# Normed tokens and their differences for the block products, moved from ScalarE and GpSimd to the vector engine, with five instead of four old-way blocks in each ConvFFN

## The chip, the cores and the metric

The kernel runs on one core of one Trainium2 chip. The metric is the device time of one execution in microseconds (us). The core's engines are TensorE (PE in the rows; PEld are its weight loads), the vector engine (DVE), ScalarE (ACT), GpSimd (POOL) and SyncE (SP), on whose queue the transfers are issued. Each engine works through its own instructions in a fixed order and waits on semaphores for the others.

## The reference, cut to what matters

Two decoder layers run over 592 tokens (16 meta tokens, 64 of samples, 512 of the prompt) of width 1024: a mixer and a ConvFFN in each. The change touches the ConvFFN:

```
u, gate = split(rms_norm(x, norm_ffn) @ w_in, 2)       # w_in: 1024 x 5632
conv = conv_b + sum(padded[:, j:j+t] * conv_w[j])      # 3 taps over time
x = x + (silu(conv) * gate) @ w_out                    # w_out: 2816 x 1024
```

## The kernel before, in words

Features lie on the 128 partitions and tokens along the free axis, so x is eight tiles of 128x592. A product in fp32 is made of three products of a high and a low part (`h`, `xl` of the tokens; `wh`, `wl` of the weights). A weight's parts are made by ScalarE (L295) and the vector engine (L299) from a tile `wr` that a transfer has filled; `wr` has two buffers, `wh` and `wl` three each.

`ffn` runs over 22 blocks of 128 features. Each makes `u` and `gate` for its features, then convolution, silu and gating (`activate`, a chain of steps that alternates between ScalarE and the vector engine).

- The *old way* (`in_block`): `dense` for u and for gate, each 8 chunks x 3 parts x 2 halves of the tokens = 48 matmuls, 96 in a block, over raw tokens; the norm's factor per token, `rb`, is multiplied in afterwards, when `up` reads the products of u (L563, L568, tile `ub`) and `gt` those of gate (L771).
- The *seven-product way* (`strassen_block`): weights and tokens are cut into quadrants, and seven products of sums and differences of quadrants take 7 x 4 x 3 = 84 matmuls. They need the normed tokens `xn` and their differences, split into high and low parts: `b11h`, `b11l`, `b2h`, `b2l` of single quadrants (`split_alone`), and of the differences (the tiles `h` and `xl` again, which the raw tokens have left by then).

Blocks 0 to `NOLD - 1` run in the old way, since the operands of the other have to be made first. Before, `NOLD` is 4: during block 1 `norm_chunk` makes `xn` (ScalarE scales by the gain, GpSimd multiplies by `rb`, L625 and L626), during block 2 `split_alone` splits single quadrants and `differences` has GpSimd subtract (L653 to L656), and after the gate products of block 3 `split_differences` splits all eight differences in one run (L662, L663). GpSimd also copies a few edge columns of each block's `ub` (`up_edges`, L545 to L549; L548 in layer 0 only) and its last columns (L554, L555); the first tap on ScalarE (L586) waits for them.

PSUM tiles of the old way come from a pool of two (`mm`), and so do the `ac` tiles of the seven-product way and those of the output projection (`out_pair`, 48 matmuls, one after each of the blocks 4 to 19): a product can start when the last but one has been read. A scheduler puts each engine's instructions in order, by the order in which the code issues them and by when their operands should be there.

Of the kernel before, what the change touches and what calls it, by code (L numbers as in the profile page):

```python
# [9 lines left out]
F32 = mybir.dt.float32  # L10
F32R = mybir.dt.float32r
I32 = mybir.dt.int32
U8 = mybir.dt.uint8
AF = mybir.ActivationFunctionType
ALU = mybir.AluOpType
# [8 lines left out]
NT = NMETA + NSAM + NP  # L24
# [75 lines left out]
def trunk_kernel(ctx: ExitStack, tc: tile.TileContext, I, O):  # L100
    nc = tc.nc
    V, S, G, T = nc.vector, nc.scalar, nc.gpsimd, nc.tensor
# [3 lines left out]
    ap = ctx.enter_context(tc.tile_pool(name="ap", bufs=1))  # L106
# [10 lines left out]
    def matmul(out, lhsT, rhs, **kw):  # L117
        n = 1
        for d in rhs.shape[1:]:
            n *= d  # L120
        m = lhsT.shape[1]
        clock[0] += max(n, 64) / 2.4 + 3 if rhs.dtype == F32R else max(2 * n, 2 * m, 64) / 1.2
        T.matmul(out, lhsT=lhsT, rhs=rhs, **kw)  # L123
# [38 lines left out]
    def tmp(name, n=NT, dt=F32):  # L162
        return tp.tile([128, n], dt, name=name, tag="t", bufs=4)
# [7 lines left out]
    def px(name):  # L171
        return pp.tile([128, 512], F32, name=name, tag="px", bufs=4)

    def mm(name):
        return pp.tile([128, 1024], F32, name=name, tag="mm", bufs=2)
# [28 lines left out]
    x = [None] * 8  # L204
    state = {"x": "xa", "h": "xb", "ssq": {}}

    def xslot(c, name, dt=F32):
        return ap.tile([128, NT], dt, name=f"{name}{c}", tag=f"{state[name]}{c}")
# [147 lines left out]
    def got(ws):  # L356
        return [sp.get() for sp in ws]
# [25 lines left out]
    def dense(ws, acts, c0=0, hooks=None, span=None):  # L383


        off, mid = OFF[c0]
        halves = [(c0, mid), (mid, NT)] if span is None else [span]
        if span is not None:
            off = -span[0]
        ps = [mm("dp") if span is None else px("dq") for _ in ws]  # L390
        nk = len(acts)
        for k in range(nk):
            xh, xl = acts[k]
            for p, (hi, lo) in zip(ps, ws):
                for i, (ww, xx) in enumerate(((hi, xh), (hi, xl), (lo, xh))):
                    for a, b in halves:
                        matmul(p[:, off + a:off + b], lhsT=ww[:, k, :], rhs=xx[:, a:b], start=k == 0 and i == 0,
                               stop=k == nk - 1 and i == 2)
            if hooks and k in hooks:
                hooks[k]()  # L400
            yield
        return ps, off
# [4 lines left out]
    def acts_x():  # L407
        return [state[c] for c in range(8)]
# [120 lines left out]
    def ffn(l, next_gain, spans=(None,)):  # L529
# [21 lines left out]
        def up_state(fc, ub):  # L551
            cvo = env["cvo"]
            ubs = ub[:, 0:100].rearrange("p (s i) -> p s i", i=10)
            G.tensor_copy(cvo[:, 0:2, fc], ub[:, 612:614])  # L554
            G.tensor_copy(cvo[:, 2:18, fc].rearrange("p (b j) -> p b j", j=2), ubs[:, 2:10, 8:10])  # L555
# [3 lines left out]
        def up(fc, pu, off):  # L559
            rb = state["rb"]  # L560
            ub = tmp("ub", 614)
            ubs = ub[:, 0:100].rearrange("p (s i) -> p s i", i=10)
            V.tensor_tensor(out=ubs[:, s0:, 2:10], in0=pu[:, off + h0:off + 80].rearrange("p (s i) -> p s i", i=8),  # L563
                            in1=rb[:, h0:80].rearrange("p (s i) -> p s i", i=8), op=ALU.mult)
            if l == 1:
                V.tensor_tensor(out=ub[:, 100:102], in0=pu[:, off + 14:off + 16], in1=rb[:, 14:16], op=ALU.mult)
            up_edges(fc, ub)
            V.tensor_tensor(out=ub[:, 102:614], in0=pu[:, off + P0:off + NT], in1=rb[:, P0:NT], op=ALU.mult)  # L568
            up_state(fc, ub)
            return ub  # L570
# [46 lines left out]
        a0 = 0 if l == 0 else 12  # L617
        n = (NT - a0) // 2
        h1, h2 = slice(a0, a0 + n), slice(a0 + n, NT)
        xn, ops = [None] * 8, {}  # L620

        def norm_chunk(c):
            g = vec[:, V_NFFN + 8 * l + c:V_NFFN + 8 * l + c + 1]
            xn[c] = ap.tile([128, NT], F32, name=f"xn{c}", tag=f"b{'hl'[c % 2]}{4 + c // 2}")
            S.activation(xn[c], x[c], AF.Copy, scale=g)  # L625
            G.tensor_tensor(out=xn[c], in0=xn[c], in1=state["rb"], op=ALU.mult)  # L626

        def split_alone(c):

            x_ = xn[c]  # L630
            if c < 4:
                if c % 2 == 0:
                    for i in "hl":
                        ops["1", i, c // 2] = tp.tile([128, 2, 296], F32R, name=f"b11{i}", tag="gate", bufs=4)
                hi, lo = (ops["1", i, c // 2][:, c % 2, 0:n] for i in "hl")
                S.activation(hi, x_[:, h1], AF.Copy, scale=-1.0)
                V.scalar_tensor_tensor(out=lo, in0=x_[:, h1], scalar=-1.0, in1=hi.bitcast(F32), op0=ALU.mult,  # L637
                                       op1=ALU.subtract)
                ops["B11", c] = (hi, lo)
            else:  # L640
                if c % 2 == 0:
                    ops["2", "h", c // 2] = ap.tile([128, 2, 592], F32R, name="b2h", tag="v", bufs=2)
                    ops["2", "l", c // 2] = tp.tile([128, 2, 592], F32R, name="b2l", tag="st", bufs=2)
                hi, lo = (ops["2", i, c // 2][:, c % 2, 0:2 * n] for i in "hl")
                S.copy(hi, x_[:, a0:NT])
                V.tensor_tensor(out=lo, in0=x_[:, a0:NT], in1=hi.bitcast(F32), op=ALU.subtract)  # L646
                ops["B21", c - 4] = (hi[:, 0:n], lo[:, 0:n])
                ops["B22", c - 4] = (hi[:, n:2 * n], lo[:, n:2 * n])

        def differences(c):  # L650

            p, q = xn[c], xn[c + 4]
            G.tensor_tensor(out=p[:, h1], in0=p[:, h1], in1=p[:, h2], op=ALU.subtract)  # L653
            G.tensor_tensor(out=p[:, h2], in0=p[:, h2], in1=q[:, h2], op=ALU.subtract)
            G.tensor_tensor(out=q[:, h2], in0=p[:, h1], in1=q[:, h2], op=ALU.add)
            G.tensor_tensor(out=q[:, h1], in0=q[:, h2], in1=q[:, h1], op=ALU.subtract)  # L656

        def split_differences():
            for c in range(8):
                hi = xslot(c, "h", F32R)  # L660
                lo = ap.tile([128, NT], F32R, name=f"xl{c}", tag=f"xl{c}")
                S.copy(hi[:, 0:2 * n], xn[c][:, a0:NT])  # L662
                V.tensor_tensor(out=lo[:, 0:2 * n], in0=xn[c][:, a0:NT], in1=hi[:, 0:2 * n].bitcast(F32),  # L663
                                op=ALU.subtract)
                a, b = ("T1", "T3") if c < 4 else ("T4", "T2")
                ops[a, c % 4] = (hi[:, 0:n], lo[:, 0:n])
                ops[b, c % 4] = (hi[:, n:2 * n], lo[:, n:2 * n])

        def strassen_block(fc):

# [74 lines left out]
            r = lambda: raw_weights([v], True)  # L745
            return (lambda: [Split(4, 256, r())], body)

        NOLD = 4

        def in_block(fc):  # L750
            def body(ww):
                hooks = (None, None)
                if fc == 0:
                    setup()
                    hooks = ({7: norm_rows}, {4: norm_bcast})
                ww = got(ww)
                if fc == 1:
                    hooks = ({k: lambda k=k: norm_chunk(k // 2 + 4 * (k % 2)) for k in range(8)}, None)
                elif fc == 2:
                    hooks = ({k: lambda k=k: split_alone(k // 2 + 4 * (k % 2)) for k in range(8)},  # L760
                             {4 + k: lambda k=k: differences(k) for k in range(4)})
                (pu,), off = yield from dense(ww[0:1], acts_x(), c0, hooks[0])
                if fc > 0:
                    ub = up(fc, pu, off)
                (pg,), off = yield from dense(ww[1:2], acts_x(), c0, hooks[1])
                if fc == 0:
                    ub = up(fc, pu, off)
                if fc == NOLD - 1:
                    split_differences()
                gt = tmp("gt")  # L770
                V.tensor_tensor(out=gt[:, h0:], in0=pg[:, off + h0:off + NT], in1=state["rb"][:, h0:], op=ALU.mult)  # L771
                activate(fc, ub, gt)
                while later:
                    step_later()

            return (lambda: weights([cols(w_in, fc * 128)], [cols(w_in, DFF + fc * 128)]), body)
# [7 lines left out]
        acts = [None] * NFC  # L784
        block = lambda fc: in_block(fc) if fc < NOLD else strassen_block(fc)
        blocks = [block(fc) for fc in range(4)]
# [919 lines left out]
```

## Time and profile before

| | |
|---|---|
| median of 3 runs | 1619.34 us (1617.38 to 1619.64) |
| the profiled execution | 1614.75 us |
| its span, first to last instruction | 1612.6 us |
| mean granted clock of TensorE | 0.986 of full speed |
| busy: PE, DVE, ACT, POOL | 95%, 72%, 46%, 16% |

Busy shares are averages over the whole span; what a stage waits for is read from that stage. A granted clock of 1.00 is the 2.4 GHz level, 0.50 the 1.2 GHz level. A row of the timeline gives the start in us, the duration in us, the engine, the line, the operation, and what it writes and reads; an instruction's duration overlaps a little with the next one's.

### The profile page before, as it was taken

To read this page: it belongs to the slowest core of one execution; us is meant where nothing else is said; L and a number is where in the kernel's file an instruction comes from. 1 tells how busy PE (TensorE), PEld (TensorE's weight loads), DVE (VectorE), ACT (ScalarE), POOL (GpSimd) and SP (SyncE) were. 2 spreads that over 40 slices of the span, in tenths; PEclk is the share of its full clock that TensorE was granted. 3 is DMA by queue.
4 is the path that set the end of the run, shared out by engine and by line. 5 is a ranking of instruction groups with operands and counts; after the bars stand their busy time and mean duration, and the time that the engine had idled before them with its cause. 6 is when DMAs were issued, how large, how long until landed. Compare 5 with 4: busy or idle time off the path is not lost. (4 is left out here: it accounts for less than half of the span.)

```text
span 1612.6 us, 32125 instructions
## 1 busy us (share of the span) xinstructions
PE 1536.5 (95%) x13076; PEld 1488.0 (92%) x13076; DVE 1166.3 (72%) x2321; ACT 743.7 (46%) x1342; POOL 251.6 (16%) x450
## 2 busy tenths in 40 slices
PE   5999999999799999999999899999998999999996
PEld 5999998999799999999999798998998999999995
DVE  6576564658798788877646867766688888888875
ACT  3543433325354444444545466564454444444453
POOL 4000000002610000011002525333035000000001
PEclk9999999999899999999999999999999999999998
DMA  5545546333132323223522122223231333223234
GB/s 149 106 84 112 83 82 88 85 123 99 40 92 79 92 88 97 79 89 90 176 79 66 55 95 75 89 90 103 94 99 53 92 92 92 89 82 105 66 107 128
DMA packets 217620, 148.55 MB, mean 92 GB/s; under 512 B 7513, under 2 KB 208985, under 8 KB 217473
## 3 DMA queue, kind: packets, MB, share of 16 engines
q1 hardware_dynamic: 217472, 146.51, 33.9%
q8 instruction: 102, 1.67, 0.4%
q14 instruction: 46, 0.37, 0.1%
HBM read 131.84 MB, written 14.65 MB: 91 GB/s over the span
## 5 line engine op out<-in xcount | busy, mean ns | idle before, releaser
L295 ACT CAST wh<-wr 128x1024 fp32r<-128x1024 f32 (+3 forms) x240 | 232.5, 970 | 383.9 <-PE dp L123 104.5
L299 DVE TENSOR_TENSOR wl<-wr,wh 128x1024 fp32r<-128x1024 f32 (+3 forms) x240 | 275.7, 1149 | 89.6 <-ACT wh L295 87.3
L123 PE MATMUL dp<-h,wh 128*128 128x296 f32 (+2 forms) x1024 | 231.4, 308 | 14.4 <-DVE ub L568 13.8
L123 PE MATMUL dp<-xl,wh 128*128 128x296 f32 (+2 forms) x1024 | 225.0, 301 | 0.0
L123 PE MATMUL dp<-h,wl 128*128 128x296 f32 (+2 forms) x1024 | 224.8, 300 | 0.0
L123 PE MATMUL dp<-bh,wh 128*128 128x296 f32 (+2 forms) x864 | 188.5, 299 | 0.8 <-DVE x L491 0.5
L123 PE MATMUL dp<-bl,wh 128*128 128x296 f32 (+2 forms) x864 | 186.3, 297 | 0.0
L123 PE MATMUL dp<-bh,wl 128*128 128x296 f32 (+2 forms) x864 | 186.3, 297 | 0.0
L123 PEld LDWEIGHTS dp<-h,wh 128*128 128x128 f32 x1024 | 166.8, 192 | 18.5 <-ACT bh L606 9.3
L123 PEld LDWEIGHTS dp<-xl,wh 128*128 128x128 f32 x1024 | 168.2, 191 | 0.0
L123 PEld LDWEIGHTS dp<-h,wl 128*128 128x128 f32 x1024 | 168.0, 191 | 0.0
L123 PEld LDWEIGHTS dp<-bh,wh 128*128 128x128 f32 x864 | 139.1, 188 | 3.1 <-issue 1.4
L123 PEld LDWEIGHTS dp<-bl,wh 128*128 128x128 f32 x864 | 139.4, 188 | 0.0
L123 PEld LDWEIGHTS dp<-bh,wl 128*128 128x128 f32 x864 | 139.2, 188 | 0.0
L123 PE MATMUL ac<-h,wh 128*128 128x296 f32 (+1 forms) x432 | 129.9, 301 | 7.7 <-ACT cs L687 4.6
L123 PE MATMUL ac<-h,wl 128*128 128x296 f32 (+1 forms) x432 | 128.6, 298 | 0.0
L123 PE MATMUL ac<-xl,wh 128*128 128x296 f32 (+1 forms) x432 | 128.1, 297 | 0.0
L123 PE MATMUL tp<-wh,h 128*128 128x256 f32 (+3 forms) x280 | 84.6, 303 | 15.6 <-ACT wh L295 10.1
L123 PEld LDWEIGHTS ac<-h,wh 128*128 128x128 f32 x432 | 81.4, 188 | 10.0 <-ACT cs L687 5.3
L595 ACT ACTIVATE cv<-cv 128x612 f32<-128x612 f32 (+1 forms) x44 | 31.1, 707 | 127.3 <-DVE cv L591 127.2
L295 ACT CAST wh<-s 128x1024 fp32r<-128x1024 f32 x72 | 60.2, 836 | 57.2 <-PE sb L123 35.0
L123 PE MATMUL sb<-b2h,wh 128*128 128x296 f32 (+1 forms) x288 | 85.9, 298 | 0.2 <-DVE ub L700 0.2
(478 smaller groups left out, 3560.9 us busy)
## 6 DMA issues: line engine op xcount, KB each, us to landing
wr<-in_w_ffn_in SPq DMA_DIRECT2D x88, 512.0 KB, 3.7
wr<-in_w_in_ab SPq DMA_DIRECT2D x32, 512.0 KB, 7.5
wr<-in_w_ffn_out SPq DMA_DIRECT2D x32, 512.0 KB, 3.4
wr<-in_w_in_c SPq DMA_DIRECT2D x32, 512.0 KB, 3.9
wr<-in_w_ffn_out SPq DMA_DIRECT2D x24, 384.0 KB, 3.5
x<-in_x SPq DMA_DIRECT2D x16, 296.0 KB, 5.6
out_H<-s_s SPq DMA_DIRECT2D x8, 576.0 KB, 4.3
wr<-in_w_out_ab SPq DMA_DIRECT2D x16, 256.0 KB, 2.9
```

Of the source, the lines that this page charges most:

```text
L123: T.matmul(out, lhsT=lhsT, rhs=rhs, **kw)
L295: S.copy(hi, src)
L299: V.tensor_tensor(out=lo, in0=src, in1=hi.bitcast(F32), op=ALU.subtract)
L595: S.activation(env_["cv"][:, b0:612], env_["cv"][:, b0:612], AF.Silu)
```

## The change

- `norm_chunk` is one step of the vector engine, which multiplies x by the gain and by `rb`.
- `differences` runs on the vector engine too, in place of GpSimd.
- `NOLD` is 5. The preparation is a list of 20 steps (8 `norm_chunk`, 8 `split_alone`, 4 `differences`), taken one at a time from hooks in the chunks of blocks 1 to 3: 6 in block 1, 10 in block 2, the last 4 in block 3.
- `split_difference` replaces `split_differences`: one chunk after each chunk of the gate products of block 4.

```
 def norm_chunk(c):
-    S.activation(xn[c], x[c], AF.Copy, scale=g)
-    G.tensor_tensor(out=xn[c], in0=xn[c], in1=state["rb"], op=ALU.mult)
+    V.scalar_tensor_tensor(out=xn[c], in0=x[c], scalar=g, in1=state["rb"], op0=ALU.mult, op1=ALU.mult)
...
 def differences(c):
-    G.tensor_tensor(out=p[:, h1], in0=p[:, h1], in1=p[:, h2], op=ALU.subtract)
...
+    V.tensor_tensor(out=p[:, h1], in0=p[:, h1], in1=p[:, h2], op=ALU.subtract)
...
-def split_differences():
-    for c in range(8):
+def split_difference(c):
...
-NOLD = 4
+NOLD = 5
+pairs = (0, 4, 1, 5, 2, 6, 3, 7)
+prep = [lambda c=c: norm_chunk(c) for c in pairs] + [lambda c=c: split_alone(c) for c in pairs]
+prep += [lambda c=c: differences(c) for c in range(4)]
+
+def prep_step():
+    if prep:
+        prep.pop(0)()
...
-    if fc == 1:
-        hooks = ({k: lambda k=k: norm_chunk(k // 2 + 4 * (k % 2)) for k in range(8)}, None)
-    elif fc == 2:
-        hooks = ({k: lambda k=k: split_alone(k // 2 + 4 * (k % 2)) for k in range(8)},
-                 {4 + k: lambda k=k: differences(k) for k in range(4)})
+    if 0 < fc < NOLD - 1:
+        hooks = ({k: prep_step for k in range(0, 8, 1 + (fc == 1))}, {k: prep_step for k in (1, 3)})
...
+    if fc == NOLD - 1:
+        hooks = (None, {k: lambda k=k: split_difference(k) for k in range(8)})
...
-    if fc == NOLD - 1:
-        split_differences()
```

What stands in a row on the vector engine in layer 0 before it reads the u products of block 1 (L563 and L568). Before:

```order
L637 SCALAR_TENSOR_TENSOR b11l<-xn_4366,b11h 128x296
L646 TENSOR_TENSOR b2l<-xn_4375,b2h 128x592
L637 SCALAR_TENSOR_TENSOR b11l<-xn_4384,b11h 128x296
L646 TENSOR_TENSOR b2l<-xn_4393,b2h 128x592
L601 TENSOR_TENSOR gt<-gt,cv 128x80
L602 TENSOR_TENSOR gt<-gt,cv 128x512
L563 TENSOR_TENSOR ub<-dp,rb 128x10x8
L568 TENSOR_TENSOR ub<-dp,rb 128x512
```

Ahead of these rows stand block 0's gate, a weight's low part, the two taps (L591), one more `b11l` and one more `b2l`. The same place after the change:

```order
L591 SCALAR_TENSOR_TENSOR cv<-ub,vec,cv 128x612
L625 SCALAR_TENSOR_TENSOR xn_4376<-x_3559,vec,rb 128x592
L625 SCALAR_TENSOR_TENSOR xn_4390<-x_3567,vec,rb 128x592
L625 SCALAR_TENSOR_TENSOR xn_4420<-x_3561,vec,rb 128x592
L601 TENSOR_TENSOR gt<-gt,cv 128x80
L602 TENSOR_TENSOR gt<-gt,cv 128x512
L563 TENSOR_TENSOR ub<-dp,rb 128x10x8
L568 TENSOR_TENSOR ub<-dp,rb 128x512
```

Six splits have left the place for five `xn` (two of them stand ahead of these rows); the splits now come behind.

The vector engine around the conversion of the differences in layer 0 (`xl`), with the gate (`gt<-dp`) of the last old-way block. Before, in front of the first reading of a seven-product block (L695):

```order
L663 TENSOR_TENSOR xl_4804<-xn_4393,h_4803 128x592
L771 TENSOR_TENSOR gt<-dp,rb 128x592
L663 TENSOR_TENSOR xl_4808<-xn_4411,h_4807 128x592
L591 SCALAR_TENSOR_TENSOR cv<-ub,vec,cv 128x612
L299 TENSOR_TENSOR wl<-wr,wh 128x1024
L591 SCALAR_TENSOR_TENSOR cv<-ub,vec,cv 128x612
L299 TENSOR_TENSOR wl<-s_4831,wh 128x512
L695 TENSOR_TENSOR ub<-sb,cs 128x10x8
```

After, in front of the first addition of the output projection to x (L738), which frees the PSUM tile that block 5 takes:

```order
L661 TENSOR_TENSOR xl_4921<-xn_4434,h_4920 128x592
L774 TENSOR_TENSOR gt<-dp,rb 128x592
L661 TENSOR_TENSOR xl_4931<-xn_4500,h_4930 128x592
L591 SCALAR_TENSOR_TENSOR cv<-ub,vec,cv 128x612
L299 TENSOR_TENSOR wl<-s_4949,wh 128x1024
L591 SCALAR_TENSOR_TENSOR cv<-ub,vec,cv 128x612
L738 TENSOR_TENSOR x_3557<-x_3557,dp 128x592
```

Six more `xl` stand ahead of either piece; an output projection, not a seven-product block, now follows them.

GpSimd in layer 0, in front of the edge copies of block 2's `ub`. Before:

```order
L653 TENSOR_TENSOR xn_4384<-xn_4384 128x296
L656 TENSOR_TENSOR xn_4375<-xn_4375 128x296
L654 TENSOR_TENSOR xn_4384<-xn_4384,xn_4393 128x296
L655 TENSOR_TENSOR xn_4393<-xn_4384,xn_4393 128x296
L656 TENSOR_TENSOR xn_4393<-xn_4393 128x296
L547 COPY ub<-ub 128x2
L548 COPY ub<-ub 128x2
```

After, at the same place:

```order
L554 COPY cvo<-ub 128x2
L545 MEMSET ub 128x2
L549 COPY ub<-cst 128x8x2
L547 COPY ub<-ub 128x2
L548 COPY ub<-ub 128x2
L555 COPY cvo<-ub 128x16
```

Only the small copies and fills of `ub` and `cvo` are left on GpSimd there.

## Rows read from the trace of the kernel before

**Rows 1.** The profile's page, part 1: busy us, share of the span, instructions.

```profile
PE 1536.5 (95%) x13076; PEld 1488.0 (92%) x13076; DVE 1166.3 (72%) x2321; ACT 743.7 (46%) x1342; POOL 251.6 (16%) x450
```

**Rows 2.** Waits of TensorE, 385 to 475 us: us in total, times, longest.

```profile
PE dp L123 <- DVE ub L568: 9.1, 2, 4.7
...
PE ac L123 <- ACT cs L687: 1.6, 1, 1.6
```

**Rows 3.** Waits of TensorE, 1190 to 1275 us.

```profile
PE dp L123 <- DVE ub L568: 4.7, 2, 4.5
...
PE ac L123 <- ACT cs L687: 3.0, 1, 3.0
```

**Rows 4.** Windows, two stages: length; PE, PEld, DVE, ACT, POOL busy (count); PEclk; DMA.

```profile
394.49:467.57 73.08, 61.58 (x420) 60.67 (x421) 60.73 (x74) 30.95 (x45) 40.06 (x50) 0.93 0.17 51
...
1198.24:1265.16 66.92, 59.26 (x421) 58.42 (x421) 60.19 (x78) 30.48 (x45) 36.10 (x37) 0.95 0.19 56
```

**Rows 5.** Windows inside layer 0's stage.

```profile
394.49:407.65 13.16, 13.16 (x96) 13.08 (x96) 13.07 (x9) 6.46 (x10) 13.16 (x9) 1.00 0.14 42
...
412.23:415.32 3.09, 3.09 (x12) 3.09 (x13) 3.09 (x3) 1.35 (x2) 3.01 (x3) 0.50 0.26 73
...
431.62:436.03 4.41, 4.41 (x18) 4.41 (x19) 0.98 (x1) 0.99 (x2) 1.21 (x3) 0.53 0.40 119
```

**Rows 6.** Windows inside layer 1's stage.

```profile
1198.24:1211.00 12.76, 12.76 (x96) 12.76 (x96) 12.66 (x9) 5.64 (x9) 12.76 (x8) 1.00 0.15 43
...
1215.72:1221.04 5.32, 5.32 (x23) 5.32 (x24) 5.32 (x6) 2.07 (x3) 5.08 (x5) 0.52 0.33 97
...
1246.86:1249.99 3.13, 0.16 (x2) 0.00 (x1) 3.13 (x6) 3.13 (x6) 0.00 (x0) 1.00 0.00 0
```

**Rows 7.** Timeline of DVE, layer 0: start us, us, instruction.

```profile
398.37 1.73 DVE L637 SCALAR_TENSOR_TENSOR b11l<-xn,b11h 128x296 fp32r<-128x296 f32 x1
...
401.99 2.04 DVE L646 TENSOR_TENSOR b2l<-xn,b2h 128x592 fp32r<-128x592 f32 x1
...
409.18 0.78 DVE L646 TENSOR_TENSOR b2l<-xn,b2h 128x592 fp32r<-128x592 f32 x1
...
411.40 0.67 DVE L568 TENSOR_TENSOR ub<-dp,rb 128x512 f32<-128x512 f32 x1
```

**Rows 8.** Timeline of DVE, layer 1.

```profile
1202.02 0.45 DVE L637 SCALAR_TENSOR_TENSOR b11l<-xn,b11h 128x290 fp32r<-128x290 f32 x1
```

**Rows 9.** Timeline of POOL, layer 0.

```profile
397.69 11.25 POOL L626 TENSOR_TENSOR xn<-xn,rb 128x592 f32<-128x592 f32 x6
```

**Rows 10.** Timeline of ACT, layer 0; in brackets the idle time ahead and its releaser.

```profile
423.78 0.90 ACT L586 ACTIVATE cv<-ub,vec 128x612 f32<-128x612 f32 x1 [10.20 <-POOL ub L548]
```

**Rows 11.** Timeline of DVE, layer 0, the last block in the old way and after.

```profile
436.27 0.69 DVE L368 TENSOR_TENSOR s<-wr 128x512 f32<-128x512 f32 x1 [3.67 <-DMA wr<-in_w_ffn_in]
...
446.44 4.88 DVE L663 TENSOR_TENSOR xl<-xn,h 128x592 fp32r<-128x592 f32 x7
```

**Rows 12.** Groups of DVE by form, 436 to 475 us: busy us, mean ns.

```profile
L299 DVE TENSOR_TENSOR wl<-wr,wh 128x1024 fp32r<-128x1024 f32 x5 | 6.1, 1219 | 0.0
...
L663 DVE TENSOR_TENSOR xl<-xn,h 128x592 fp32r<-128x592 f32 x8 | 5.6, 766 | 0.0
...
L591 DVE SCALAR_TENSOR_TENSOR cv<-ub,vec,cv 128x612 f32<-128x612 f32 x6 | 5.1, 848 | 0.0
...
L368 DVE TENSOR_TENSOR s<-wr 128x512 f32<-128x512 f32 x3 | 2.1, 687 | 4.1 <-DMA wr<-in_w_ffn_in 4.1
...
L741 DVE TENSOR_TENSOR x<-x,dp 128x592 f32<-128x592 f32 x2 | 1.5, 766 | 0.4 <-PE dp L123 0.4
...
L721 DVE TENSOR_TENSOR gt<-cs,ac 128x296 f32<-128x296 f32 x1 | 0.5, 464 | 0.0
```

**Rows 13.** Groups of POOL by form, 394 to 432 us.

```profile
L655 POOL TENSOR_TENSOR xn<-xn,xn 128x296 f32<-128x296 f32 x4 | 5.6, 1405 | 0.3
...
L656 POOL TENSOR_TENSOR xn<-xn 128x296 f32<-128x296 f32 x4 | 3.7, 922 | 0.2
```

More of the change, by code (lines that the diff above doesn't have):

```diff
@@ L652, in differences @@
             p, q = xn[c], xn[c + 4]
-            G.tensor_tensor(out=p[:, h1], in0=p[:, h1], in1=p[:, h2], op=ALU.subtract)
-            G.tensor_tensor(out=p[:, h2], in0=p[:, h2], in1=q[:, h2], op=ALU.subtract)
-            G.tensor_tensor(out=q[:, h2], in0=p[:, h1], in1=q[:, h2], op=ALU.add)
-            G.tensor_tensor(out=q[:, h1], in0=q[:, h2], in1=q[:, h1], op=ALU.subtract)
-        def split_differences():
-            for c in range(8):
[L660 to L667, printed above, removed]
+            V.tensor_tensor(out=p[:, h1], in0=p[:, h1], in1=p[:, h2], op=ALU.subtract)
+            V.tensor_tensor(out=p[:, h2], in0=p[:, h2], in1=q[:, h2], op=ALU.subtract)
+            V.tensor_tensor(out=q[:, h2], in0=p[:, h1], in1=q[:, h2], op=ALU.add)
+            V.tensor_tensor(out=q[:, h1], in0=q[:, h2], in1=q[:, h1], op=ALU.subtract)
+        def split_difference(c):
+            hi = xslot(c, "h", F32R)
+            lo = ap.tile([128, NT], F32R, name=f"xl{c}", tag=f"xl{c}")
+            S.copy(hi[:, 0:2 * n], xn[c][:, a0:NT])
+            V.tensor_tensor(out=lo[:, 0:2 * n], in0=xn[c][:, a0:NT], in1=hi[:, 0:2 * n].bitcast(F32), op=ALU.subtract)
+            a, b = ("T1", "T3") if c < 4 else ("T4", "T2")
+            ops[a, c % 4] = (hi[:, 0:n], lo[:, 0:n])
+            ops[b, c % 4] = (hi[:, n:2 * n], lo[:, n:2 * n])
         def strassen_block(fc):
```

## The prediction

> **What bounds the kernel now.** I read the page's busy line first [rows 1]: TensorE is busy 95% of the span, so the time is TensorE's own work plus its idle stretches and the stretches at a low clock. The waits of TensorE over the two places where the diff acts then name what it lacked. In the first ConvFFN it waits twice, 9.1 us in all, for `ub` (L568, the vector engine's last read of a PSUM tile), then 1.6 us for the copy `cs` inside the first block that uses seven products [rows 2]. In the second ConvFFN the longest wait for `ub` is 4.5 us, and that for `cs` 3.0 us [rows 3]. The windows show the price: the stage from block 1's first product to block 5's first takes 73.08 us in layer 0 and 66.92 us in layer 1, both with 420 or 421 matmuls [rows 4]. A block without disturbance takes 13.16 us for 96 matmuls (0.1371 us each) in layer 0 [rows 5] and 12.76 us (0.1329 us each) in layer 1 [rows 6]. So 420 matmuls should take 57.6 and 55.8 us: 15.5 and 11.1 us are lost. Part of the loss is clock: after the long waits 12 matmuls take 3.09 us and 18 take 4.41 us at a granted clock of about 0.5 (the 1.2 GHz level) [rows 5], and 23 take 5.32 us in layer 1 [rows 6]; at full rate these are 1.65, 2.47 and 3.06, so 1.4 + 1.9 + 2.3 us. After the 3.13 us wait the clock row stays at 1.00 [rows 6].
>
> **Why `ub` is late.** The vector engine's rows of that time show one instruction at two prices: `b2l` 128x592 takes 2.04 us at 401.99, 0.78 us at 409.18; `b11l` takes 1.73 us at 398.37 [rows 7] and 0.45 us in layer 1 [rows 8]. The slow ones lie beside GpSimd's multiplications of `xn` (six in 11.25 us from 397.69 [rows 9]); the 0.78 us one begins when these are over, and the 0.45 us one in a gap between two of layer 1's. `ub`, which reads PSUM, takes 0.67 us with GpSimd busy [rows 7]. So slow splits, taps and weight parts put `ub` behind by several us. The second wait of layer 0 has another path: ScalarE stands 10.20 us for GpSimd's edge copy L548 [rows 10], which is queued behind the differences on GpSimd. All lost stretches but the last ones thus hang on the GpSimd work that the change removes.
>
> **The change part by part.**
> 1. *One block more in the old way per layer.* 96 matmuls instead of 84. In the same stage (block 1 to the first product of block 5) there are then 432 matmuls instead of 420. Cost if nothing waits: 12 x 0.1371 + 12 x 0.1329 = 3.2 us. This lies on the path in full, since TensorE is the bound.
> 2. *`xn` on the vector engine.* The sixteen scalings leave ScalarE (they ran early, beside the output projection, and nothing waited for them), the multiplications leave GpSimd. The vector engine gets 8 steps of 128x592 per layer; not in the trace with these operands. Nearest rows: seven `xl` of 128x592 in 4.88 us, 0.70 us each [rows 11], below; the tap of 128x612, the same kind of step, 0.85 us [rows 12], above. I take 0.76: 6.1 us per layer.
> 3. *Differences.* 16 of 128x296 per layer at 0.46 us [rows 12], of which some 0.08 us overlap with the next (0.77 a row, 0.70 start to start, for `xl`): 0.38, 6.1 us per layer.
> 4. *The splits lose their slow half.* Four `b11l` and four `b2l` per layer at 0.45 and 0.78 instead of 1.7 and 2.0 us: about 8 to 10 us of the vector engine's time come back, nearly as much as 2 and 3 together add (12.2 us).
> 5. *The conversions `xl` move* from one run of eight at the start of the first seven-product block into the second half of block 4, each behind TensorE's last read of that chunk. Queued behind them are the gate of block 4, its taps, a weight's low part and the first `x` addition; the output projection's 48 matmuls follow block 4, so these have 6.5 us more than before.
> 6. *DMA.* The second weight half of block 5 goes to a buffer that block 4's frees; its sum waited 3.67 us before [rows 11] with nobody else waiting. The order of SP's queue is unchanged, and the sum is due a block later. I cost it at nothing; its cover is block 4's gate half, about 6.5 us.
>
> **Does the vector engine fit?** Following the order in the new program from 394.3 us with the prices above, between `ub` of block 0 and `ub` of block 1 stand five `xn`, one gate, one weight part, two taps and two gate products: 8.6 us, so `ub` of block 1 is read at about 402.9; TensorE needs it at 407.65. For blocks 2 and 3 I get 415 and 429.5 against 420.7 and 433.8. ScalarE's tap for block 1 no longer has GpSimd's differences in front. The tight place is the end: from the last product of block 4's first half to the `x` addition that frees the PSUM tile of block 5 stand 17 instructions on the vector engine, 12.3 us (7 x 0.70 for `xl`, 2 x 1.14 for weights, the rest as above); TensorE has 96 matmuls there, 13.16 us [rows 5]. ScalarE's copies for `xl` may add some 0.5 us, an estimate. The margin is 0.4 to 0.9 us in layer 0, and about the same in layer 1. In the stage as a whole the vector engine's load is, by the rows [rows 12]: four blocks at 7.5 us (two weight parts 1.22, two taps 0.85, gate and low part 0.77 each, two reads or products of 512 at 0.69, two small ones of some 0.2), block 5's four sums 2.7, the output projection 2 x 0.77 + 1.22, eight `xn` 6.7, splits 1.8 + 3.1, differences 7.3, `xl` 6.1: 60.5 us. These 87 instructions overlap by 0.07 us each (as `xl` does), so 54.4 us of 59.2 are taken, 92%.
>
> **The sum.** If no wait is left: layer 0 73.08 - 432 x 0.1371 = 13.9 us, layer 1 66.92 - 432 x 0.1329 = 9.5 us; together 23.4 us, the extra matmuls included. I leave 0.5 us for the tight place: 22.9 us. The profiled execution took 1614.75 us, 4.6 us below the median 1619.34; nothing in the sum scales with that, so I take it off both: 1591.9 beside the profile, **1596.4 us** beside the median. Block rates without the small hiccup at the head of block 1 would give up to 1 us more.
>
> **Rivals.**
> *A new wait at the end of block 4.* The `x` addition or the last `xl` comes late, and TensorE waits before block 5. For it: 92% load and a margin below 1 us; `h` and `xl` now wait for TensorE chunk by chunk, with everything queued behind them. Against it: no long instruction stands there. Its price is read from waits at such a place: 1.6 and 3.0 us, with the clock at 1.00, give 3 to 6 us over the two layers, 1599 to 1603; if they grow to the 4.5 us kind, with 1.4 to 2.3 us of clock behind each, about 13 us: 1609.
> *The work is no cheaper on the vector engine.* This ends slower. If the moved steps cost there what they cost GpSimd (1.87 us a multiplication [rows 9], 0.92 to 1.41 us a difference [rows 13], take 1.13), the vector engine's load is 54.4 + 8 x 1.11 + 16 x 0.75 = 75.3 us a layer, it becomes the bound, and the stages take 2.2 and 8.4 us more than today: 1630. It decides from about 70 us, where each of the 24 moved steps costs 0.65 us more than I take. Against it: the fast rows 0.78 and 0.45 us at moments when GpSimd was out of the way [rows 7, 8], and `xl`, two operands in SBUF, at 0.70 with ScalarE busy beside it [rows 11].
> The Trainium skill (Perfetto Trace Analysis, section Optimizing Scalar/DVE Operations) speaks for this rival: GpSimd and the vector engine share a read port, so moving work between the two might not help. By that rule the time would be that of this rival; rows 7 show the sharing, but also that the price falls to less than half as soon as one of the two is idle.
> *Only the waits change places.* If the first block's `ub` were still late because five `xn` now stand in front of it, the gain would be the extra matmuls short of zero: about 1619. `ub` is late at all only if an `xn` takes 1.7 us or more, so I give this little.
>
> **How the numbers follow.** Forecast case (all waits but a trace gone, 1593 to 1599): 0.72. New wait (1599 to 1609): 0.20, of which about three quarters below 1605. No change: 0.03. Slower (1622 to 1640): 0.05. The range from 1593 to 1605 holds the first case and most of the second. About 0.2%, 3.2 us, is what a measurement of this kernel can tell from no change: faster 0.92, same 0.03, slower 0.05.
>
> **What would show it.** In the new profile: no wait of TensorE for `ub` in either ConvFFN; PEclk at 1.00 through both stages; 24 matmuls more; `b11l` and `b2l` at about 0.45 and 0.78 us; GpSimd's busy time down by 50 us or more; `xn` at 0.7 to 0.85 us; the stages near 59 and 57 us. `xn` at 1.5 us or more, or a wait over 2 us before block 5 in both layers, would make the prediction wrong.

## The result, and the profile after

The changed kernel takes 1591.02 us (median of 4 runs, 1588.79 to 1593.28) beside 1618.36 us for the kernel before (4 runs, 1614.02 to 1619.64). The ratio on record is 0.9856, 95% interval 0.9832 to 0.988. The quotient of the two medians would be 0.9831, but three of the four runs before are the older ones behind the 1619.34 us of the section on the time before; beside the fourth, 1614.02 us, the quotient is 0.9858. Two later comparisons of the same pair gave 0.9852 [0.983, 0.9873] and 0.986 [0.9838, 0.9882]. The forecast, 1596.4 of 1619.34, is a ratio of 0.9858: by these ratios the gain was forecast as it came. The time itself lies 5.4 us under the forecast and 2 us under the low end of the range; why, stands below.

First the page's busy line of the changed kernel, which answers to [rows 1].

```profile
PE 1537.6 (97%) x13100; PEld 1489.0 (94%) x13100; DVE 1153.5 (72%) x2351; ACT 729.0 (46%) x1316; POOL 208.3 (13%) x402
```

TensorE has 24 matmuls more and is busy 97% of a shorter span (1591.4 us). Then the two stages, from block 1's first product to block 5's first, in the columns of [rows 4]: length; busy us of PE, PEld, DVE, ACT, POOL; PEclk; DMA share; GB/s.

```profile
390.64:449.55 58.91, 58.91 (x432) 58.91 (x433) 55.44 (x91) 29.33 (x41) 15.02 (x27) 1.00 0.25 73
1184.60:1242.00 57.40, 57.40 (x432) 57.30 (x433) 54.76 (x94) 28.77 (x41) 12.81 (x14) 1.00 0.25 74
```

TensorE's busy time equals the length of the stage in both, at a granted clock of 1.00. Against [rows 4] the stages are 14.17 and 9.52 us shorter, 23.69 together. TensorE has no wait at all in the view from 385 to 470 us, where [rows 2] had 9.1 us for `ub` alone. These are all its waits from 1150 to 1270 us (total, times, longest):

```profile
PE dp L123 <- DVE ub L568: 0.2, 1, 0.2
PE rbp L123 <- DVE dg L269: 0.2, 1, 0.2
```

The vector engine's groups by form in layer 0 (busy us, mean ns) show the moved steps and those that had been slow. First two groups of the kernel before, 388 to 432 us, then, behind the dots, the changed kernel, 386 to 432 us:

```profile
L646 DVE TENSOR_TENSOR b2l<-xn,b2h 128x592 fp32r<-128x592 f32 x4 | 6.2, 1561 | 0.0
L637 DVE SCALAR_TENSOR_TENSOR b11l<-xn,b11h 128x296 fp32r<-128x296 f32 x4 | 6.2, 1559 | 0.0
...
L625 DVE SCALAR_TENSOR_TENSOR xn<-x,vec,rb 128x592 f32<-128x592 f32 x8 | 6.4, 832 | 0.0
...
L645 DVE TENSOR_TENSOR b2l<-xn,b2h 128x592 fp32r<-128x592 f32 x4 | 3.1, 772 | 0.0
...
L636 DVE SCALAR_TENSOR_TENSOR b11l<-xn,b11h 128x296 fp32r<-128x296 f32 x4 | 1.9, 463 | 0.0
...
L653 DVE TENSOR_TENSOR xn<-xn,xn 128x296 f32<-128x296 f32 x4 | 1.8, 459 | 0.0
```

`b2l` took 2.04 us in [rows 7], 1.56 in the mean of its four, and now 0.77; `b11l` took 1.73, 1.56 in the mean, and now 0.46. The new `xn` has 0.83 us in its row.

### The profile page after: what moved, and what is told of

It reads as the page before. It is cut to its first block, busy times and chain, and to the rows that moved or that the text cites. A ratio compares the mean times of both kernels' runs of the same rounds, so it can differ in the third digit from the quotient of the medians.

```text
span 1591.4 us, 32114 instructions
## 1 busy us (share of the span) xinstructions
PE 1537.6 (97%) x13100; PEld 1489.0 (94%) x13100; DVE 1153.5 (72%) x2351; ACT 729.0 (46%) x1316; POOL 208.3 (13%) x402
## 3 DMA queue, kind: packets, MB, share of 16 engines
q8 instruction: 103, 1.69, 0.4%
## 5 line engine op out<-in xcount | busy, mean ns | idle before, releaser
L123 PE MATMUL dp<-h,wh 128*128 128x296 f32 (+1 forms) x1088 | 242.3, 304 | 0.7 <-ACT v_c L918 0.5
L123 PE MATMUL dp<-h,wl 128*128 128x296 f32 (+1 forms) x1088 | 236.7, 298 | 0.0
L123 PE MATMUL dp<-xl,wh 128*128 128x296 f32 (+1 forms) x1088 | 236.6, 298 | 0.0
L123 PEld LDWEIGHTS dp<-h,wh 128*128 128x128 f32 x1088 | 174.9, 189 | 4.3 <-issue 1.8
L123 PEld LDWEIGHTS dp<-h,wl 128*128 128x128 f32 x1088 | 176.4, 189 | 0.0
L123 PEld LDWEIGHTS dp<-xl,wh 128*128 128x128 f32 x1088 | 176.2, 189 | 0.0
L123 PE MATMUL ac<-h,wh 128*128 128x296 f32 (+1 forms) x408 | 123.8, 303 | 3.0 <-DVE cs L704 2.7
L123 PE MATMUL ac<-h,wl 128*128 128x296 f32 (+1 forms) x408 | 121.5, 298 | 0.0
L123 PE MATMUL ac<-xl,wh 128*128 128x296 f32 (+1 forms) x408 | 121.1, 297 | 0.0
L123 PE MATMUL tp<-wl,h 128*128 128x256 f32 (+3 forms) x280 | 81.7, 292 | 0.3 <-DVE wl L299 0.3
```

## The experiments

All but the two repeats are built from one of the two kernels by the few lines shown. Beside the whole time I measure two distances in each layer: from the last product into `rbp` (1.56 us ahead of block 1's first product in both kernels) to the first product of block 5 and to that of block 6. Block 6 is done with seven products in every kernel here, so its column holds the price of a further old-way block too.

| kernel | time us (runs) | before, same comparison | L0: block 5 / 6 | L1: block 5 / 6 |
|---|---|---|---|---|
| before | 1618.36 (4) | | 74.64 / 92.60 | 68.48 / 86.06 |
| changed | 1591.02 (4) | 1618.36 | 60.47 / 78.44 | 58.96 / 76.96 |
| e0_changed_again | 1588.95 (4) | 1613.84 | 60.43 / 78.40 | 58.96 / 77.09 |
| e0_changed_third | 1591.61 (4) | 1613.06 | 60.41 / 78.38 | 58.94 / 76.96 |
| e1_fifth_block_alone | 1613.28 (1) | 1613.84 | 73.40 / 91.43 | 67.71 / 85.65 |
| e2_engines_alone | 1591.70 (4) | 1613.84 | 61.71 / 79.67 | 62.40 / 80.54 |
| e3_xn_alone | 1600.41 (1) | 1613.51 | 65.05 / 83.03 | 64.61 / 82.22 |
| e4_differences_alone | 1607.23 (1) | 1613.51 | 66.44 / 84.49 | 66.03 / 84.02 |
| e5_four_low_parts_twice | 1587.34 (1) | 1613.51 | – / 79.92 | – / 78.07 |
| e6_gpsimd_beside | 1607.77 (1) | 1613.51 | 67.95 / 86.01 | 65.14 / 83.27 |
| e8_six_blocks | 1596.26 (1) | 1613.84 | – / 80.01 | – / 78.11 |
| e10_gpsimd_memsets | 1592.26 (1) | 1613.06 | 60.53 / 78.47 | 59.31 / 77.26 |
| e11_four_blocks_sums_early | 1593.71 (1) | 1613.06 | 62.49 / 80.46 | 62.35 / 79.94 |
| e12_four_blocks_weights_early | 1591.86 (4) | 1613.06 | 60.86 / 79.50 | 60.15 / 78.73 |

A single time moves by some us from run to run (the changed kernel alone from 1586.2 to 1593.4). The distances of the changed kernel agree within 0.06 us to block 5 and 0.13 us to block 6 over three profiles, so verdicts on a few us go by them.

**The repeats.** The changed kernel ran again beside the other groups, with no edit.

> The changed kernel once more, for the comparison with the others on one chip: 22 to 27 us faster than the kernel before; stages from block 1 to block 5 of 58.9 and 57.4 us; no wait for ub over 0.5 us.

> The changed kernel for the comparison on one chip: 24 us faster than the kernel before, give or take 3; no wait of TensorE over 0.3 us in the two stages.

The gains by the medians were 24.9 and 21.5 us, after 27.3 in the first comparison, which counts three older runs of the kernel before. It is the kernel before that moved most: 1618.36, 1613.84 and 1613.06.

**The fifth block alone.** The kernel before, with one more block in the old way.

```
-        NOLD = 4
+        NOLD = 5
```

> The kernel before with five old-way blocks in place of four; ScalarE and GpSimd still make the normed tokens and the differences. Theory (GpSimd's work beside the vector engine and its queue make the waits): both waits for ub in layer 0 (4.4 and 4.7 us) and the one in layer 1 (4.5 us) are back with their low clock behind them, only the waits for cs go; 24 matmuls more; the time within 5 us of the kernel before. Rival (the fifth block's room is what brought the gain): no wait over 1 us, 20 us or more faster.

The time was 1613.28 beside 1613.84, no gain. TensorE's waits of more than 0.5 us in layer 0, 370 to 480 us:

```profile
PE dp L123 <- DVE ub L568: 8.9, 2, 4.6
```

The wait for `cs` in [rows 2] has gone, the two for `ub` stand as they were. To block 6 the layers gain 1.17 and 0.41 us: what the waits for `cs` gave back, the further matmuls mostly took. In layer 1 new waits of 1.0 and 0.6 us took some as well. The late `ub` thus doesn't depend on whether four or five blocks are done in the old way.

**The engines alone.** The kernel before, with four blocks and its old preparation, and `xn` and the differences as steps of the vector engine.

```
-            S.activation(xn[c], x[c], AF.Copy, scale=g)
-            G.tensor_tensor(out=xn[c], in0=xn[c], in1=state["rb"], op=ALU.mult)
+            V.scalar_tensor_tensor(out=xn[c], in0=x[c], scalar=g, in1=state["rb"], op0=ALU.mult, op1=ALU.mult)
...
-            G.tensor_tensor(out=p[:, h1], in0=p[:, h1], in1=p[:, h2], op=ALU.subtract)
+            V.tensor_tensor(out=p[:, h1], in0=p[:, h1], in1=p[:, h2], op=ALU.subtract)
...
```

> The kernel before with the normed tokens and the differences made by the vector engine, four old-way blocks, the old hooks and one run of split differences. Theory: all the waits for ub are gone as in the changed kernel, and 24 matmuls are saved against it; by the order of its instructions and the prices of the changed kernel's trace the vector engine just fits (the second weight of block 4 about 0.1 us before it is due), so it is 1 to 3 us faster than the changed kernel. Rival (the fifth block is needed): a wait of 3 us or more in or before block 4 in each layer, slower than the changed kernel by 3 us or more.

It gave 1591.70 beside 1588.95 for the changed kernel on the same chip: nearly the whole gain. By the distances to block 6 it stands 1.27 and 3.45 us behind that run of the changed kernel, where I had expected it ahead, though it has 24 matmuls fewer. The waits say where (in layer 1 the granted clock falls behind them as well, to 0.66 in the mean from 1227 to 1232 us); first layer 0 (370 to 480 us), then, behind the dots, layer 1 (1150 to 1290 us):

```profile
PE sd L123 <- ACT wh L295: 1.6, 1, 1.6
PE ac L123 <- DVE wl L299: 0.3, 1, 0.3
...
PE sd L123 <- ACT wh L295: 2.6, 1, 2.6
PE ac L123 <- DVE wl L299: 0.3, 1, 0.3
```

No `ub` is late any more. The wait has moved into the first seven-product block, for a weight. The timeline of the vector engine, and behind the dots that of ScalarE, name the chain:

```profile
424.75 4.88 DVE L662 TENSOR_TENSOR xl<-xn,h 128x592 fp32r<-128x592 f32 x7
429.55 0.77 DVE L770 TENSOR_TENSOR gt<-dp,rb 128x592 f32<-128x592 f32 x1
430.23 0.68 DVE L372 TENSOR_TENSOR wr<-wr 128x512 f32<-128x512 f32 x1
...
430.95 1.05 ACT L295 CAST wh<-wr 128x1024 fp32r<-128x1024 f32 x1 [1.96 <-DVE wr L372]
```

The weight's sum (L372) is queued on the vector engine behind seven `xl` and a gate; ScalarE stands 1.96 us for it. With the engine this full, the order of its work decides.

**One half of the moved work at a time.** The changed kernel, with the differences back on GpSimd (e3, the four lines of the form `-V.tensor_tensor`, `+G.tensor_tensor`), or with `xn` back on ScalarE and GpSimd (e4, the first three lines of e2's diff the other way round).

```
 def differences(c):
-            V.tensor_tensor(out=p[:, h1], in0=p[:, h1], in1=p[:, h2], op=ALU.subtract)
+            G.tensor_tensor(out=p[:, h1], in0=p[:, h1], in1=p[:, h2], op=ALU.subtract)
...
```

> The changed kernel with the differences back on GpSimd; the normed tokens stay on the vector engine. Theory: the wait for ub of block 1 is gone in both layers (xn at 0.75 us); in layer 0 ScalarE waits for an edge copy behind the 16 differences, and TensorE waits 3 to 5 us once in blocks 2 to 4; layer 1 loses less. Stages about 64 to 66 us in layer 0 and 57 to 60 in layer 1. Rival (the differences' place does not matter): 59 and 57 us as in the changed kernel.

> The changed kernel with the normed tokens made by ScalarE and GpSimd again; the differences stay on the vector engine. Theory: GpSimd's multiplications stand beside the vector engine in blocks 1 and 2 again, its two-operand steps take 1.7 to 2.0 us there, and the wait for ub of block 1 is back at 3 to 5 us in both layers with a low clock behind it; no wait behind edge copies. Stages about 65 and 64 us. Rival: 59 and 57 us.

Putting the differences back costs 4.6 + 5.3 = 9.9 us to block 6, putting `xn` back costs 6.1 + 7.1 = 13.1 us. Together that is 23.0, nearly the 23.3 us by which the changed kernel leads to block 6 (178.66 against 155.40 us, both layers). The parts do not simply add, though: counted from the kernel before, the fifth block alone (e1) gains 1.6 us, the engine moves alone (e2) 18.5, and both with the new order 23.3. The waits of TensorE in layer 0, with the differences back and, behind the dots, with `xn` back:

```profile
PE dp L123 <- DVE gt L774: 3.0, 1, 3.0
...
PE dp L123 <- DVE ub L568: 3.8, 1, 3.8
PE ac L123 <- ACT cv L595: 0.3, 1, 0.3
```

With `xn` back the first long wait for `ub` returns (4.41 us in the kernel before, 3.82 here) and the second does not, as expected. With the differences back I had looked for the wait in another place, and for less loss in layer 1, where the stage took some 63 us and not 57 to 60: it is block 4's gate `gt` that comes late, in front of the output projection's second half. One reading, not tested by itself, is a backlog. The vector engine stood 3.95 us for a weight's transfer, ahead of block 3's gate (435.23). From there on it is idle for only 0.8 us before it comes to seven `xl` and, behind them, to the gate that TensorE waits for (448.87):

```profile
433.89 0.69 DVE L368 TENSOR_TENSOR s<-wr 128x512 f32<-128x512 f32 x1 [3.95 <-DMA wr<-in_w_ffn_in]
...
435.23 0.77 DVE L774 TENSOR_TENSOR gt<-dp,rb 128x592 f32<-128x592 f32 x1
...
444.07 4.88 DVE L661 TENSOR_TENSOR xl<-xn,h 128x592 fp32r<-128x592 f32 x7
448.87 0.77 DVE L774 TENSOR_TENSOR gt<-dp,rb 128x592 f32<-128x592 f32 x1
```

The price of a split follows its neighbour on GpSimd. By form, layer 0: `b2l` and `b11l` with the differences on GpSimd (386 to 440 us), and behind the dots with `xn` there (386 to 432 us):

```profile
L645 DVE TENSOR_TENSOR b2l<-xn,b2h 128x592 fp32r<-128x592 f32 x4 | 5.0, 1242 | 0.0
L636 DVE SCALAR_TENSOR_TENSOR b11l<-xn,b11h 128x296 fp32r<-128x296 f32 x4 | 3.8, 940 | 0.0
...
L637 DVE SCALAR_TENSOR_TENSOR b11l<-xn,b11h 128x296 fp32r<-128x296 f32 x4 | 5.6, 1407 | 0.0
L646 DVE TENSOR_TENSOR b2l<-xn,b2h 128x592 fp32r<-128x592 f32 x4 | 5.6, 1401 | 0.0
```

**GpSimd made busy beside the changed kernel.** Sixteen further multiplications of 128x296 per layer on GpSimd, into a tile that nothing reads; the vector engine's program is the same.

```
 def norm_chunk(c):
+            gsc = ap.tile([128, 296], F32, name="gsc", tag="gsc")
+            for k in (0, 296):
+                G.tensor_tensor(out=gsc, in0=x[c][:, k:k + 296], in1=state["rb"][:, k:k + 296], op=ALU.mult)
```

> The changed kernel with extra GpSimd work that nothing uses: for each normed tile two multiplications of 128x296 into a scratch tile. Theory (GpSimd slows the vector engine's steps that read two operands from SBUF): xn at 1.3 us or more in place of 0.75 while GpSimd is busy, ub of block 1 late, waits of TensorE of 2 us or more in both layers. Rival (the order on the engines was the cause, not the neighbourhood): xn at 0.75 us, no wait except one behind GpSimd's edge copies in layer 0.

It took 1607.77 us, and stands 7.6 + 6.3 = 13.9 us behind the changed kernel at block 6. GpSimd's own small copies now queue behind the added work, and the vector engine stood 1.1 us for a `cv` in layer 0 in turn; but no price of a step comes from a queue. TensorE waits in layer 0 for `ub` 1.8 us in two pieces, less than I had expected, and longest for the gates (total, times, longest). Behind the dots stand rows of the vector engine beside the added work, and one of that work (`gsc`):

```profile
PE dp L123 <- DVE gt L777: 3.9, 2, 2.3
...
393.28 0.82 DVE L625 SCALAR_TENSOR_TENSOR xn<-x,vec,rb 128x592 f32<-128x592 f32 x1
393.36 1.44 POOL L628 TENSOR_TENSOR gsc<-x,rb 128x296 f32<-128x296 f32 x1
...
395.38 3.46 DVE L625 SCALAR_TENSOR_TENSOR xn<-x,vec,rb 128x592 f32<-128x592 f32 x3
...
400.31 0.68 DVE L568 TENSOR_TENSOR ub<-dp,rb 128x512 f32<-128x512 f32 x1
...
404.74 2.70 DVE L625 SCALAR_TENSOR_TENSOR xn<-x,vec,rb 128x592 f32<-128x592 f32 x2
...
408.38 1.39 DVE L648 TENSOR_TENSOR b2l<-xn,b2h 128x592 fp32r<-128x592 f32 x1
409.69 0.76 DVE L777 TENSOR_TENSOR gt<-dp,rb 128x592 f32<-128x592 f32 x1
```

Three `xn` in 3.46 us take 2.32 in the changed kernel, and `b2l` 1.39 instead of 0.77. `ub` and the gate `gt`, which read PSUM, keep their 0.68 and 0.76. So GpSimd's multiplications slow the steps whose two tensors both lie in SBUF, though not each of them: `xn` at 393.28 took 0.82 us, and it is the multiplication that started 0.08 us behind it that took 1.44, where one by itself (at 387.58) took 0.83. Of these two, the step that started first kept its price. How much of the 13.9 us is due to these prices and how much to the copies is not separated. The mean of all eight `xn` is 1169 ns, under the 1.3 us expected, since not all of them met a multiplication that was under way. A second form of this test, with fills that read nothing, leaves open whether fills slow the vector engine: all 96 of them were placed between 1.8 and 62.9 us, far ahead of the stages, and the distances stayed within 0.35 us of the changed kernel's.

```
 def norm_chunk(c):
+            gsc = ap.tile([128, 296], F32, name="gsc", tag="gsc")
+            for _ in range(6):
+                G.memset(gsc, 0.0)
```

> The changed kernel with extra GpSimd work that only writes: for each normed tile six fills of 128x296 of a scratch tile. If GpSimd's mere activity slows the vector engine, xn stands at 1.1 us or more as with the extra multiplications and TensorE waits; if only its reads do, xn stays at 0.83 us a row and TensorE waits for nothing except perhaps behind GpSimd's edge copies in layer 0.

**How tight is the end of block 4?** The changed kernel, with four of the eight `xl` made twice.

```
-            V.tensor_tensor(out=lo[:, 0:2 * n], in0=xn[c][:, a0:NT], in1=hi[:, 0:2 * n].bitcast(F32), op=ALU.subtract)
+            for _ in range(2 if c < 4 else 1):
+                V.tensor_tensor(out=lo[:, 0:2 * n], in0=xn[c][:, a0:NT], in1=hi[:, 0:2 * n].bitcast(F32), op=ALU.subtract)
```

> The changed kernel with the first four low parts of the differences made twice: 2.8 us more on the vector engine between block 4's first half and the x addition that frees block 5's tile. Theory (this is the tight place; in the trace of the changed kernel the addition ends 0.28 us before TensorE needs it in layer 0 and just as it needs it in layer 1): waits of TensorE of about 2.5 and 2.8 us before block 5, 5 us slower. Rival (there is more room): no wait, the same time.

Some 2.8 us of work a layer (four at 0.70) cost 1.48 and 1.11 us to block 6, about half of what the theory had. The whole time was 1587.34, within the changed kernel's own runs. A part is covered because the order changed too: the twelve `xl` run from 436.51 for 8.31 us, and TensorE does block 5's `sb` products in the middle of the output projection, until the gate is there:

```profile
443.15 0.29 PE L123 MATMUL sb<-b2h,wh 128*128 128x296 f32 x1
...
445.56 0.54 PE L123 MATMUL dp<-bh,wh 128*128 128x296 f32 x2 [0.62 <-DVE gt L775]
```

So the test doesn't give the margin cleanly; it does show that the end of block 4 has little to spare.

**Six blocks.** The changed kernel with one more block in the old way.

```
-        NOLD = 5
+        NOLD = 6
```

> The changed kernel with six old-way blocks. Theory (nothing is left to wait for, so an old-way block costs its 12 extra matmuls in full): 24 matmuls more than the changed kernel, at 0.136 and 0.133 us, so 3.2 us slower than it and no new wait. Rival (the vector engine is still short of room): within 1 us or faster.

To block 6 it costs 1.57 + 1.15 = 2.7 us, where 12 matmuls a layer at the rates of [rows 5, 6] are 3.2. TensorE has no wait in layer 0 and one of 0.2 us in layer 1. That is the price of an old-way block when it hides nothing.

**Four blocks, in a better order.** The changed kernel with four old-way blocks and a preparation step at every chunk of block 1 too, the sums of weights taken ahead of `xl` (e11), and in e12 the weight of `u` given back as soon as its products are read, so that the next weight's parts are made earlier.

```
-        NOLD = 5
+        NOLD = 4
...
-                    hooks = ({k: prep_step for k in range(0, 8, 1 + (fc == 1))}, {k: prep_step for k in (1, 3)})
+                    hooks = ({k: prep_step for k in range(8)}, {k: prep_step for k in (1, 3)})
...
+                    for sp in line:
+                        sp.sum_up()
...
-                ww = got(ww)
+                ws, ww = ww, got(ww)
...
+                    ws[0].done()
```

> As the run with four blocks and early weights, but only the sums are made ahead, not the second weight's parts. Theory (order): the wait for the third weight goes, one of 1 to 2.5 us for the second weight's low part stands in its place. Rival (time): the sum of the waits in block 4 as with the engine moves alone, 1.9 us in layer 0 and 3 us in layer 1.

> The changed kernel with four old-way blocks again (hooks for the preparation in blocks 1 and 2, the differences split chunk by chunk in block 3), and in block 3 the next block's weight sums and its second weight's parts made ahead of the split differences. Theory (the fifth block only buys the vector engine time that its order can buy as well): the waits of 1.6 and 2.6 us for the third weight in block 4 fall below 1 us, block 5 starts 1.4 to 1.6 us earlier than in the changed kernel in each layer less what is left of the waits; 0 to 3 us faster than it. Rival (the vector engine is short of time, not of order): 2 us or more of waits in block 4 in each layer, 1 to 4 us slower than the changed kernel.

e11 took 1593.71 us and stands 2.0 and 3.0 us behind the changed kernel at block 6. The wait for the third weight has gone and 0.2 and 1.0 us for the second weight's low part stand in its place, but TensorE also waits 1.4 us for `cs` in each layer, which neither theory nor rival had named. e12 has 1591.86 us (ratio 0.9869 [0.9855, 0.9884]) beside 1591.61 for the changed kernel on the same chip: the same. At block 6 it is 1.06 and 1.77 us behind, where the theory had it up to 3 us ahead. Its waits over 0.2 us in layer 0, and behind the dots in layer 1, are all inside the first seven-product block and the one after:

```profile
PE ac L123 <- ACT cs L684: 1.3, 1, 1.3
PE ac L123 <- DVE cs L704: 0.4, 1, 0.4
...
PE sb L123 <- DVE ub L697: 0.7, 1, 0.7
PE ac L123 <- DVE cs L704: 0.7, 1, 0.7
PE ac L123 <- ACT cs L684: 0.7, 1, 0.7
PE sd L123 <- DVE xl L661: 0.5, 1, 0.5
```

The fifth block costs 2.7 to 3.2 us and buys the time in which the vector engine and ScalarE make what e2, e11 and e12 wait for; against a better order of four blocks that comes out about even. No kernel here is clearly faster than the changed one.

## Why the prediction was right, and where not

**The diagnosis held.** That slow splits beside GpSimd put `ub` behind was read from one instruction at two prices [rows 7, 8]. e1 shows that the block count does not touch it, e2 that the engine moves alone remove it, e4 brings the first of the waits back, and e6 brings the slow prices back with unused work. One reading was too simple: the fast `b11l` of [rows 8] does not lie in a gap of GpSimd's work, but started 0.08 us ahead of a multiplication (1202.10, 1.69 us); as in the pair of rows of e6, the step that started first kept its price. The second wait of layer 0 I had put down to the differences that stand on GpSimd ahead of an edge copy [rows 10], which is that of block 1's `ub`, not of block 2's as the section on the change calls it. That was half of it: it stays away with the differences moved (e4), but also with `xn` alone moved (e3). There `ub` of block 1 is early enough that its edge copy (398.99) stands ahead of the first difference (403.99); before, 12 of the 16 differences stood ahead of it. The wait needed both on GpSimd.

**The prices held.** `xn` was taken at 0.76 from start to start; three in a row now take 2.32 us, 0.75 from start to start. The differences, in two pairs, 0.83 us for two, so 0.38 as taken. The stage's load on the vector engine was put at 54.4 us; it is 55.44 and 54.76, 94 and 95% of the stage where I said 92. What is left free in layer 0 lies nearly all in one piece: 3.14 us, in which the engine waits for the products of block 3's gate (430.58). From there to block 5 it has no pause. One term was too high: item 4 had all eight splits at the slow price, 8 to 10 us to come back, but some were fast before, and in layer 0 their sum fell from 12.4 to 5.0 us, by 7.4. Taps and weight parts had slow rows as well (2.05 us at 400.02, 2.35 at 395.33) and gave back time too.

**The step through blocks 1 to 3 held.** `ub` of block 1 was to be read 8.6 us after 394.3. In the changed kernel, whose stage begins 3.85 us earlier, this row is 8.0 us after 390.4:

```profile
390.41 0.83 DVE L625 SCALAR_TENSOR_TENSOR xn<-x,vec,rb 128x592 f32<-128x592 f32 x1
...
398.39 0.69 DVE L568 TENSOR_TENSOR ub<-dp,rb 128x512 f32<-128x512 f32 x1
...
410.72 0.68 DVE L568 TENSOR_TENSOR ub<-dp,rb 128x512 f32<-128x512 f32 x1
...
425.61 0.69 DVE L568 TENSOR_TENSOR ub<-dp,rb 128x512 f32<-128x512 f32 x1
```

For blocks 2 and 3 I had 415 and 429.5, which with the shift are 411.2 and 425.7; the rows say 410.72 and 425.61.

**The sum held.** 13.9 and 9.5 us were forecast from the rates of [rows 5, 6], 14.17 and 9.52 came. The 0.5 us taken off for the tight place was not needed, but it was no empty worry: the `x` addition that frees block 5's tile ends at 449.27, and block 5 starts at 449.55. In layer 1 the row below ends 0.14 us ahead of 1242.00. I had put the margin at 0.4 to 0.9 us; it is 0.28 and 0.14. In layer 0 the 17 steps take 12.18 us from the first `ub` row below, where I had counted 12.3. The 0.5 us for ScalarE's copies is a term that no run shows: seven `xl` follow each other in 4.89 us without idle time. But block 3's gating (L602, 436.49) stands ahead of the 17 steps, so they begin 0.6 us after block 4's second half, which starts at 436.50; the count had left that out.

```profile
437.09 0.24 DVE L563 TENSOR_TENSOR ub<-dp,rb 128x80 f32<-128x80 f32 x1
...
448.49 0.78 DVE L738 TENSOR_TENSOR x<-x,dp 128x592 f32<-128x592 f32 x1
...
1241.11 0.75 DVE L738 TENSOR_TENSOR x<-x,dp 128x576 f32<-128x576 f32 x1
```

**The DMA item held.** The weight half whose sum stood 3.67 us in [rows 11], then block 4's and now block 5's, is summed at 431.27 directly behind block 3's gate, with no wait.

**The rival at the end of block 4 did not come**, but it was near: e2 and e12 have their waits of 0.3 to 2.6 us right behind that place, e3 has 3.0 us in front of it. **That only the waits change places did not come either:** the one wait for `ub` that is left is 0.2 us in layer 1, where [rows 3] had 4.7. **That the work might be no cheaper on the vector engine is refuted** by 0.83 us a row for `xn` against GpSimd's 1.87 us a multiplication [rows 9]. The Trainium skill (Perfetto Trace Analysis, section Optimizing Scalar/DVE Operations) warns that moving work between GpSimd and the vector engine might not help. Here e6 shows the two engines slowing each other, and the runs show that ending this helped: e2 alone took 18.5 us off the two layers to block 6.

**The absolute time was missed by the last step of the sum**, which took the gain off 1619.34 us, the median of three runs that later runs did not repeat, and put the low end of the range at 1593 without room for the scatter of that median. Later runs put the kernel before at 1614.02 us (one run) and, as medians of seven, at 1613.84 and 1613.06. The profiled execution, off which I had put 1591.9 us, came at 1593.28; the difference is found outside the stages. From the start of the span to layer 0's stage it is 3.85 us shorter than before, between the stages 4.38 longer and behind them 1.96 longer, 2.5 us in all. In the middle, 2.2 us of it is a spell of low clock which the profile of before does not have (below).

**One number was wrong:** GpSimd's busy time fell by 43.3 us, not 50 or more. The moved steps had taken 64.2 us in the two layers, but the 44 copies of 128x2 (L554) grew from 15.7 to 36.7 us over the whole span. Five of them took 4.2 us in layer 0's stage before, and now:

```profile
L554 POOL COPY cvo<-ub 128x2 f32<-128x2 f32 x5 | 11.4, 2271 | 1.5 <-DVE ub L568 1.1
```

No engine's late work follows from it: TensorE has no wait in that stage.

## What to carry to other kernels

If one instruction of the vector engine shows two prices in a trace, look at what GpSimd does in the slow ones; work moved from GpSimd then costs its fast price and gives back the slow halves of its neighbours, here some 12 us of work a layer for 18.5 us of time in the two layers (e2), and 23.3 with the fifth block and the new order. Such a move fills the engine (94% here), and from there the order of its queue decides what is late next, as the weight behind seven `xl` in e2. Forecast a ratio and leave room for the scatter of the median that it is applied to.

## What the runs showed of the hardware that I had not expected

**GpSimd's small copies suffer as well.** The longest copy of 128x2 on GpSimd took 6.60 us (its usual time is 0.19). First its row, then the vector engine's rows of the same time:

```profile
437.99 6.60 POOL L554 COPY cvo<-ub 128x2 f32<-128x2 f32 x1
...
439.66 4.89 DVE L661 TENSOR_TENSOR xl<-xn,h 128x592 fp32r<-128x592 f32 x7
444.45 0.78 DVE L774 TENSOR_TENSOR gt<-dp,rb 128x592 f32<-128x592 f32 x1
```

It ends at 444.59, just after the gate, which reads PSUM, has begun. That it waited for a gap between steps with two tensors in SBUF fits the rows; it was not tested by itself. In e6 a multiplication got its turn between two such steps in a row (it started at 405.58 and ended at 406.81, while two `xn` ran from 404.74 to 407.44), so why this copy waited through nine steps stays open.

**The clock falls in one run and not in the next at the same place of the program.** A stretch of layer 1's mixer in the changed kernel and, behind the dots, the same products in the kernel before (from `pl<-ex,kd` to the next `pl<-ex`), in the columns of [rows 4]:

```profile
970.43:976.05 5.62, 5.62 (x32) 5.37 (x31) 2.39 (x4) 2.90 (x6) 3.29 (x6) 0.55 0.44 158
...
986.32:989.73 3.41, 3.41 (x31) 3.21 (x30) 1.95 (x3) 1.73 (x4) 3.41 (x7) 1.00 0.57 193
```

The same products take 5.62 us at a granted clock of 0.55 and 3.41 us at 1.00; the two repeats of the changed kernel take 3.40 and 3.42 us, at 1.00. Around its start TensorE was busy 4.13 us of 5 (965 to 970 us, where the mean clock is already 0.86) in the one and 4.15 (981 to 986 us, 1.00) in the other, with the same two short waits of 0.5 and 0.3 us. Another place, near 275 us, shows the same: its 10 us have a granted clock of 0.66 in the changed kernel and 1.00 in the first repeat, with TensorE busy 6.81 and 7.03 us. The mean granted clock of the three profiles is 0.989, 0.993 and 0.990, their spans are 1591.4, 1585.2 and 1590.9 us, while their distances to block 6 agree within 0.13 us.
